# A hybrid decoder step: who issues two groups of loads, a second mask buffer, and where three small pieces of work stand in the order

## The chip, the cores and the metric

The kernel runs on one core of a Trainium2 chip. Its engines are TensorE (PE, matmuls; PEld is its loading of weights), VectorE (DVE), ScalarE (ACT), GpSimd (POOL) and SyncE (SP), which only starts transfers (DMAs). Each engine executes its own instructions in order, and waits where one needs what another engine or a transfer has not delivered. PE, DVE, ACT and POOL work on tiles in on-chip memory; `dram` names and the names ending in S or D (`qS`, `usD`, `biasS`) are buffers in device memory.

The metric is the device time of one execution in microseconds (us); of several runs the median is taken. From one further execution there is a profile: a record of every instruction with its start, its length and what it waited for.

## The reference

One layer of a decoder with two kinds of heads, for a prompt of 1024 tokens and 8 single decode tokens with a paged cache of 4096 positions each (R = 1032 columns in all, model width D = 2048), in float32:

```python
h = rmsnorm(x)
p = h @ w_in                        # q, k, v, index q/k/weights, gates, mLSTM q/k/v ...
# sparse attention: every query keeps its 256 best keys by an index score
s = relu(einsum('bqhd,bld->bqlh', qi, ki))        # 16 index heads of 64
scores = einsum('bqlh,bqh->bql', s, wi) * IDX_SCALE
_, idx = top_k(where(causal, scores, -inf), 256)
att = softmax(q @ k[idx] * ATT_SCALE) @ v[idx]    # 8 heads, 2 KV heads of 128
# mLSTM heads: chunks of 64 tokens, state C (256 x 128), n, m for each of 4 heads
h_ml, C, n, m = mlstm_run(...)
mix = concat(att * silu(z_att), rms(h_ml) * w * sigmoid(o) * silu(z_ml))
y = rmsnorm(x + mix @ w_out) * final_norm_w
```

The 8 decode tokens do the same against keys gathered from the cache. The outputs are y, the new keys and values, and the mLSTM states.

## The kernel before

**Tiles and products.** A float32 product is made of three matmuls on a high and a low part of each operand (H and L): H·H, H·L and L·H. `wH` is a weight tile rounded to the short format (made by ACT, line 251), `wL` the remainder (by DVE, line 252); `wraw` is the weight as loaded. Some of the input projection, and the output projection, are done as 7 products of 2x2 blocks in place of 8, for which sums and differences of weight blocks and of activations are formed first.

**Stages**, by the trace's time. Up to some 180 us: activations are loaded, normalised and split, and the first columns projected. To 390 us: the value columns (matmuls of line 1579, weights of lines 1573 to 1575). To 955 us: the other columns (matmuls `pj` of line 1509, results taken over by DVE into `ev` at line 375 or 377). To 1640 us: gates, products with the pre-summed weights (line 1746) and mLSTM. Then the output projection, whose last part (from 1760 us) is the blocks of line 2096.

**Jobs beside the projection.** Between the matmuls of a column the loop steps three *lanes* of jobs. A job is a generator that yields a weight after each small piece of work, and `Lane.step` paces it so that it ends by its due time (counted in columns). What a job emits stands in program order among the projection's instructions; a scheduler may move instructions, those passed to `pin` keep their place. The change touches these:

- `job_index` (from line 457) computes index scores and picks the best 256. It loads the index queries in groups of four heads, a *quad* (`qi`, line 471: 24 loads of 256 KB, two buffers); PE multiplies them by the index keys `ki` (line 489), ACT applies the relu (line 491, tile `rl`, two buffers), DVE sums the heads into `s` (line 494). For two blocks of 128 queries at a time, a search over 31 bits finds the threshold (lines 527 to 550). Then a mask is made for each block q = 0, 1 (lines 554 to 566): `gt` for scores above, `eq` for equal ones, a scan that keeps the first of these, and the store of `gt` to `biasS`.
- `job_dscore` gathers the decode tokens' index keys from the cache: POOL issues 32 gathers `kp` (line 1001, three buffers), PE transposes and multiplies them (line 1023).
- `job_datt` (from line 1263) is the attention of the decode tokens: gathers `ck` and `cv` on POOL (line 1289); for each of 8 tokens two products with the query (DVE, line 1314), each followed by a reduction (line 1318).
- `job_usum` (lines 1418 to 1431) forms weight sums in device memory for 12 pairs of columns: four sums `usD[0..3, i]` for each pair i. SP copies a block (line 1424), then POOL issues a transfer that adds another block to it (line 1425). Sum 1 starts from a copy of sum 0, and sum 2 from a copy of sum 1. Four pairs run side by side, step by step.

`gate_stage` reads the sums with the loads of lines 1728 and 1733.

**Last stage.** For the weight blocks' sums POOL computes `tt` (line 2090 in `tsum`), ACT and DVE split them (lines 2080 and 2085), and the activations are split by lines 2006 and 2007. Small work is put into a list `late`, of which `spread` emits some entries after each step k: among them `square` (line 2116, a sum of squares of finished rows) and `scaled` (line 2123: POOL multiplies finished rows `yt` by the norm's weight `fnr`).

Of the kernel before, what the change touches and what calls it, by code (L numbers as in the profile page):

```python
# [8 lines left out]
F32 = mybir.dt.float32  # L9
F32R = mybir.dt.float32r  # L10
BF16 = mybir.dt.bfloat16
I32 = mybir.dt.int32
AF = mybir.ActivationFunctionType
OP = mybir.AluOpType
# [4 lines left out]
S = 1024  # L19
# [32 lines left out]
T_G = 37  # L52
# [6 lines left out]
NP = (NT - T_G) // 2  # L59
# [112 lines left out]
def body(tc, A, stop=None):  # L172
# [284 lines left out]
    def job_index(groups):  # L457
        with tc.tile_pool(name="ix", bufs=2) as px:
# [6 lines left out]
            qis = {}  # L465

            def load_q(n):
                if n < len(quads):
                    i, h = quads[n]
                    qis[n] = px.tile([128, 4, 128], F32R, name="qi", bufs=2)  # L470
                    SY.dma_start(qis[n].bitcast(F32), qv[:, h:h + 4, i * 128:(i + 1) * 128])

            nq = 0
            load_q(0)
# [2 lines left out]
            for blocks in groups:  # L477
# [73 lines left out]
                V.tensor_tensor(tf, Tt.bitcast(F32), sgn, OP.mult)  # L551
                for q, i in enumerate(blocks):
                    W = (i + 1) * 128
                    gt = px.tile([128, S], BF16, name="gt", bufs=1)
                    eq = px.tile([128, S], BF16, name="eq", bufs=1)
                    s = Sv[q]
                    V.tensor_scalar(gt[:, :W], s[:, :W], sgn[:, q:q + 1], tf[:, q:q + 1], OP.mult, OP.is_gt)
                    V.tensor_scalar(eq[:, :W], s[:, :W], sgn[:, q:q + 1], tf[:, q:q + 1], OP.mult, OP.is_equal)
                    V.tensor_reduce(cnt[:, q:q + 1], gt[:, :W], AX.X, OP.add)
                    V.tensor_scalar(kp[:, q:q + 1], cnt[:, q:q + 1], -1.0, float(TOPK), OP.mult, OP.add)  # L560
                    yield W * 3.5
                    pin(V.tensor_tensor_scan(s[:, :W], eq[:, :W], eq[:, :W], 0.0, OP.add, OP.bypass))
                    V.scalar_tensor_tensor(eq[:, :W], s[:, :W], kp[:, q:q + 1], eq[:, :W], OP.is_le, OP.mult)
                    V.tensor_tensor(gt[:, :W], gt[:, :W], eq[:, :W], OP.add)
                    V.tensor_scalar(gt[:, :W], gt[:, :W], -1.0, POS, OP.add, OP.mult)
                    SY.dma_start(biasS[i], gt[:, :W])
                    yield W * 3.5
# [695 lines left out]
    def job_datt():  # L1263
        with tc.tile_pool(name="da", bufs=1, side="right") as pd:
# [41 lines left out]
            for b in range(NB):  # L1306
                if b + 2 < NB:
                    kgs.append(gather("ck", b + 2))
                if b + 2 < NB:
                    qbs.append(qload(b + 2))  # L1310
                qb, kg = qbs.pop(0), kgs.pop(0)
                for u in range(2):
                    jk = pd.tile([128, 8, 128], F32, name="jk", bufs=1)
                    v = V.tensor_tensor(jk.rearrange("p (v h) d -> p v h d", v=2),
                                    kg[u].rearrange("p (v d) -> p v d", v=2).unsqueeze(2).to_broadcast([128, 2, 4, 128]),
                                    qb.rearrange("p (v h) d -> p v h d", v=2), OP.mult)
                    pin(v)
                    V.tensor_reduce(lT[:, u, b * 8:b * 8 + 8], jk, AX.X, OP.add)
                V.tensor_tensor(kn[:, b, :].rearrange("p (v h) -> p v h", v=2),
                                dec[:, T_AQ:T_AQ + 8, b].rearrange("p (v h) -> p v h", v=2),  # L1320
                                dec[:, T_AK:T_AK + 2, b].unsqueeze(2).to_broadcast([128, 2, 4]), OP.mult)
                if b > 4:
                    vgs.append(gather("cv", b - 5))
                yield 5000
            for _ in range(4):
                yield 6000
            p2 = bank()
# [90 lines left out]
    def job_usum():  # L1418
        def steps(i):
            c1, c2 = T_G + 2 * i, T_G + 2 * i + 1  # L1420
            b11, b21 = (A["wa"][c1 - 9, y:y + 2] for y in (0, 2))
            b12, b22 = (A["wa"][c2 - 9, y:y + 2] for y in (0, 2))
            for n, base, more in ((0, b11, b12), (3, b22, b12), (1, usD[0, i], b22), (2, usD[1, i], b21)):
                yield lambda n=n, b=base: SY.dma_start(usD[n, i], b)
                yield lambda n=n, m=more: G.dma_start(usD[n, i], m, accum_op=OP.add, max_dma_last_dim=8192)  # L1425

        for i4 in range(0, NP, 4):
            for fs in zip(*(list(steps(i)) for i in range(i4, i4 + 4))):
                for f in fs:
                    pin(f())  # L1430
                    yield 1

    def att_free():
        return "datt" in lanes[1].done and "k" in mlc
# [7 lines left out]
    def ix_weight(blocks):  # L1442
# [13 lines left out]
                   Job("qrows", T_MQ + 0.5, 31, 1, job_qrows),  # L1456
                   Job("datt", T_MQ, T_G + 0.5, 10000 + 8 * 5000 + 34000 + 5 * 2500 + 8000 + 8000 + 5000, job_datt, ix_free),
                   Job("dml", T_G, T_G + 13, 28000 + 16 * 2500 + 5000, job_dml, dml_free)]),
             Lane([Job("usum", 19, T_G - 3, 8 * NP, job_usum)])]
    gateV = gateS.rearrange("(k p) r -> k p r", p=128)  # L1460
    mixb = [None] * KT
    first = []
# [685 lines left out]
    late = []  # L2148
    pw = None

    def spread(n):
        for f in late[:n]:
            f()
        del late[:n]
# [57 lines left out]
    def rows3(f, bs, g, tie=True):  # L2212
        late.extend(lambda b=b: f(b, g, True) if tie else f(b, g) for b in bs)
# [3 lines left out]
    for n in range(2):  # L2217
        ps = banks3(n)
        for k in range(8):
            with tc.high_priority():  # L2220
                T_ = tsplit(wblock(1, n, k, *single(n, k)), None, n > 0)
            blocks(ps, k, sP2[k], T_, LOW)
            spread(2)
            if not n and k < 4:
                pairprep(k)
            if n and k % 2:
                pairprep(4 + k // 2)
        for b in LOW:
            late.append(add(yt[b][n], ps[b], yt[b + HB * n][n]))
        if not n:  # L2230
            rows3(square, LOW, 0)
            rows3(scaled, LOW, 0)
    spread(9)

    sP7 = [None] * 8
# [1 line left out]
    for n in range(2):  # L2237
        p6, p4 = banks3(0), banks3(1)
        for k in range(8):
            with tc.high_priority():  # L2240
                b12 = wblock(0, 2 + n, k, pt, 6)
                b11 = wblock(0, n, k, pt, 6)
                b22 = wblock(1, 2 + n, k, pt, 6)
                b21 = wblock(1, n, k, wst, 2)
                t1 = tsum(b12, b11, G)
                SY.dma_start(t1D[n, k], t1)
                t2 = tsum(b22, t1, G)
                T2 = tsplit(t2, None, True)
                T4 = tsplit(tsum(T2[2], b21, V, OP.subtract, bank()))
            blocks(p6, k, pairs[k][0], T2, LOW)  # L2250
            blocks(p4, k, pairs[k][1], T4, LOW)
            spread(2)
            if n and k < 4:
                with tc.high_priority():
                    for j in (2 * k, 2 * k + 1):
                        sP7[j] = ssplit(quad(j)[0])
        with tc.high_priority():
            for b in LOW:
                V.tensor_tensor(yt[b][2 + n], p6[b], yt[b + HB][n], OP.add)
            for b in LOW:  # L2260
                V.tensor_tensor(yt[b + HB][n], yt[b][2 + n], p4[b], OP.subtract)
# [143 lines left out]
```

## Time and profile before

| | us |
|---|---|
| runs | 1994.36, 1994.91, 2005.22 |
| median | 1994.91 |
| profiled execution, its own time | 2002.27 |
| span of its instructions | 2000.1 |
| mean granted clock of TensorE, as a share of full speed | 0.986 |

| engine | busy us | instructions |
|---|---|---|
| PE | 1931.4 | 12710 |
| DVE | 1435.0 | 3280 |
| ACT | 900.7 | 1864 |
| POOL | 496.5 | 542 |

The span runs from the first to the last instruction. How a line of the profile is read: `L489` is line 489 of the kernel; `bank<-ki,qi` names what is written and what is read; `x2` is a count. In the list of waits, `A <- B: 11.1, 3, 4.7` says that A waited for B for 11.1 us in all, 3 times, 4.7 at the longest. In a time line the first number is the start, the second the length, and `[4.71 <-DMA qi<-qS]` says that the engine stood idle for 4.71 us before it and what ended that. `SPq` is SP's queue of transfers to be started: the length there is that of the starting, not of the transfer. "DMA to landing" is the time from the issue of a transfer to its end.

### The profile page before, as it was taken

To read this page: it belongs to the slowest core of one execution; us is meant where nothing else is said; L and a number is where in the kernel's file an instruction comes from. 1 tells how busy PE (TensorE), PEld (TensorE's weight loads), DVE (VectorE), ACT (ScalarE), POOL (GpSimd) and SP (SyncE) were. 2 spreads that over 40 slices of the span, in tenths; PEclk is the share of its full clock that TensorE was granted. 3 is DMA by queue.
4 is the path that set the end of the run, shared out by engine and by line. 5 is a ranking of instruction groups with operands and counts; after the bars stand their busy time and mean duration, and the time that the engine had idled before them with its cause. 6 is when DMAs were issued, how large, how long until landed. Compare 5 with 4: busy or idle time off the path is not lost. (4 is left out here: it accounts for less than half of the span.)

```text
span 2000.1 us, 35984 instructions
## 1 busy us (share of the span) xinstructions
PE 1931.4 (97%) x12710; PEld 1830.6 (92%) x12710; DVE 1435.0 (72%) x3280; ACT 900.7 (45%) x1864; POOL 496.5 (25%) x542
## 2 busy tenths in 40 slices
PE   9999998999999999989999999999999999998997
PEld 9998877899989899989899999999999999987886
DVE  8444888666858777867455658776778586788787
ACT  8122554345304345301155546554655444454655
POOL 0576776022310110033100000002123131106533
PEclk9999999999999999999999999999999999999999
DMA  7567565445875876387733597767789868898875
GB/s 259 149 196 209 172 186 158 124 155 181 242 206 153 216 195 164 101 237 223 228 98 99 164 300 215 231 192 244 230 252 318 205 240 271 271 344 280 278 253 191
DMA packets 250290, 421.31 MB, mean 211 GB/s; under 512 B 40101, under 2 KB 117221, under 8 KB 246269
## 3 DMA queue, kind: packets, MB, share of 16 engines
q1 hardware_dynamic: 231149, 347.68, 55.0%
q0 software_dynamic: 17664, 69.57, 13.9%
q8 instruction: 100, 1.64, 0.3%
q10 hardware_dynamic: 1296, 1.77, 0.3%
q14 instruction: 81, 0.66, 0.1%
HBM read 333.76 MB, written 135.48 MB: 235 GB/s over the span
## 5 line engine op out<-in xcount | busy, mean ns | idle before, releaser
L1509 PE MATMUL pj<-xH,wH 128*128 128x344 f32 (+1 forms) x1200 | 391.1, 329 | 14.1 <-DVE ev L375 8.7
L1509 PE MATMUL pj<-xL,wH 128*128 128x344 f32 (+1 forms) x1200 | 390.6, 326 | 0.2 <-DVE xL L309 0.2
L1509 PE MATMUL pj<-xH,wL 128*128 128x344 f32 (+1 forms) x1200 | 390.0, 326 | 0.0
L1746 PE MATMUL pj<-xH 128*128 128x258 f32 x1152 | 329.3, 286 | 2.5 <-DVE ev L1832 2.5
L1746 PE MATMUL pj<-xH,xL 128*128 128x258 f32 x1152 | 329.0, 286 | 0.0
L1746 PE MATMUL pj<-xL,xH 128*128 128x258 f32 x1152 | 328.7, 286 | 0.0
L1509 PEld LDWEIGHTS pj<-xH,wH 128*128 128x128 f32 x1200 | 227.6, 190 | 18.2 <-issue 13.9
L251 ACT CAST wH<-wraw 128x512 fp32r<-128x512 f32 (+2 forms) x183 | 109.9, 610 | 286.1 <-PE pj L1509 180.6
L1509 PEld LDWEIGHTS pj<-xL,wH 128*128 128x128 f32 x1200 | 227.9, 190 | 2.0 <-DVE xL L309 0.7
L1509 PEld LDWEIGHTS pj<-xH,wL 128*128 128x128 f32 x1200 | 227.8, 190 | 1.0
L1746 PEld LDWEIGHTS pj<-xH 128*128 128x128 f32 x1152 | 219.2, 190 | 5.3 <-issue 4.7
L1746 PEld LDWEIGHTS pj<-xL,xH 128*128 128x128 f32 x1152 | 219.2, 190 | 1.7 <-issue 0.4
L1746 PEld LDWEIGHTS pj<-xH,xL 128*128 128x128 f32 x1152 | 219.0, 190 | 1.8 <-issue 0.8
L252 DVE TENSOR_TENSOR wL<-wraw,wH 128x512 fp32r<-128x512 f32 (+2 forms) x183 | 129.7, 719 | 95.4 <-ACT wH L251 94.0
L538 ACT ACTIVATE eq<-eq 128x512 bf16<-128x512 bf16 (+2 forms) x93 | 78.5, 844 | 131.8 <-DVE eq L537 131.8
L2096 PE MATMUL pj<-wH,sH 128*128 128x512 f32 x336 | 131.2, 391 | 0.8 <-ACT wH L2080 0.4
L2096 PE MATMUL pj<-wH,sL 128*128 128x512 f32 x336 | 130.8, 389 | 0.0
L2096 PE MATMUL pj<-wL,sH 128*128 128x512 f32 x336 | 125.3, 392 | 4.9 <-DVE wL L2085 4.9
L491 ACT ACTIVATE rl<-bank 128x512 f32<-128x512 f32 (+2 forms) x160 | 80.1, 524 | 102.1 <-PE bank L489 67.0
L494 DVE SCALAR_TENSOR_TENSOR s<-rl,wiN,s 128x512 f32<-128x512 f32 (+2 forms) x150 | 101.9, 699 | 24.5 <-ACT rl L491 21.8
L1425 POOL DMA_DIRECT2D usD<-in_wa_dram x48 | 40.6, 1051 | 287.1 <-DMA usD<-in_wa_dram 169.7
L882 POOL CAST aH<-onec 128x4 fp32r<-128x4 f32 x16 | 6.0, 373 | 399.2 <-DVE onec L821 399.2
(506 smaller groups left out, 4828.9 us busy)
## 6 DMA issues: line engine op xcount, KB each, us to landing
wraw<-in_wt_dram SPq DMA_DIRECT2D x144, 256.0 KB
wraw<-in_wa_dram SPq DMA_DIRECT2D x110, 256.0 KB
usD<-in_wa_dram POOLq DMA_DIRECT2D x48, 512.0 KB, 8.5
wraw<-in_wo_dram SPq DMA_DIRECT2D x64, 256.0 KB
usD<-in_wa_dram SPq DMA_DIRECT2D x24, 512.0 KB
usD<-usD SPq DMA_DIRECT2D x24, 512.0 KB
xL<-xsD SPq DMA_DIRECT2D x40, 258.0 KB
ev<-spD SPq DMA_DIRECT2D x38, 258.0 KB
```

Of the source, the lines that this page charges most:

```text
L251: a = SC.copy(H[:, s, :cols], raw[:, s, :cols])
L252: return a, V.tensor_tensor(L[:, s, :cols], raw[:, s, :cols], H[:, s, :cols].bitcast(F32), OP.subtract)
L491: SC.activation(r[:, :cn], p[:, :cn], AF.Relu)
L494: v = V.scalar_tensor_tensor(s[:, c0:c0 + cn], r[:, :cn], wv, s[:, c0:c0 + cn], OP.mult, OP.add)
L538: SC.activation(junk2[:, :W1], junk2[:, :W1], AF.Copy, accum_out=cnt[:, 1:2])
L882: G.tensor_copy(aH[:, :, 256:258], onec)
L1425: yield lambda n=n, m=more: G.dma_start(usD[n, i], m, accum_op=OP.add, max_dma_last_dim=8192)
L1509: m = PE.matmul(ps[:cols, :cn], w_[:, k, :cols], x_[kk][:, c0:c0 + cn], start=(kk == ends[0] and z == 0), stop=(kk == ends[1] and z == 2))
L1746: PE.matmul(ps[c], w_[:, q, ks], x[y][:, c * CS:c * CS + CS], start=(first and q == 0 and k == 0 and z == 0), stop=(q == 1 and k == 3 and ...
L2096: PE.matmul(ps[b], S_[x][:, b * 128:b * 128 + 128], T_[y], start=(k == 0 and z == 0), stop=(k == 7 and z == 2))
```

## The change

Five edits. Lines behind 1312 move down by up to 12 in the new file, so that line 1424's copies are line 1427 there, line 1425's sums line 1430, and line 2123 is line 2134.

1. The 24 index-query loads are issued by ACT (`SC`) instead of SP (`SY`).
2. The mask of the second block of a pair is kept in the ring of the relu's output (`rl`, two buffers) instead of the single buffer `gt`.
3. In `job_datt` one yield of 5000 for each token becomes two of 2500, the first behind the first product and reduction.
4. In `job_usum` the copies of one sum to the next are issued by POOL (`G`) instead of SP, one pair behind; pairs follow each other instead of running four side by side. The job is due one column sooner.
5. In the last stage the scaling of the first finished rows is put into the list behind step 3 of the next loop instead of ahead of that loop.

```diff
@@ job_index
-                    SY.dma_start(qis[n].bitcast(F32), qv[:, h:h + 4, i * 128:(i + 1) * 128])
+                    SC.dma_start(qis[n].bitcast(F32), qv[:, h:h + 4, i * 128:(i + 1) * 128])
@@
-                    gt = px.tile([128, S], BF16, name="gt", bufs=1)
+                    gt = px.tile([128, S], BF16, name="rl" if q else "gt", bufs=1 + bool(q))
@@ job_datt
                     V.tensor_reduce(lT[:, u, b * 8:b * 8 + 8], jk, AX.X, OP.add)
+                    if not u:
+                        yield 2500
...
-                yield 5000
+                yield 2500
@@ job_usum
-            for n, base, more in ((0, b11, b12), (3, b22, b12), (1, usD[0, i], b22), (2, usD[1, i], b21)):
-                yield lambda n=n, b=base: SY.dma_start(usD[n, i], b)
-                yield lambda n=n, m=more: G.dma_start(usD[n, i], m, accum_op=OP.add, max_dma_last_dim=8192)
-
-        for i4 in range(0, NP, 4):
-            for fs in zip(*(list(steps(i)) for i in range(i4, i4 + 4))):
-                for f in fs:
+
+            def copy(n, src, queue):
+                return lambda: queue.dma_start(usD[n, i], src)
+
+            def plus(n, src):
+                return lambda: G.dma_start(usD[n, i], src, accum_op=OP.add, max_dma_last_dim=8192)
+
+            return ([copy(0, b11, SY), plus(0, b12), copy(3, b22, SY), plus(3, b12)],
+                    [copy(1, usD[0, i], G), plus(1, b22), copy(2, usD[1, i], G), plus(2, b21)])
+
+        late = []
+        for i in range(NP + 1):
+            now, more = steps(i) if i < NP else ([], [])
+            for n in range(4):
+                for f in now[n:n + 1] + late[n:n + 1]:
                     pin(f())
                     yield 1
+            late = more
@@ lanes
-             Lane([Job("usum", 19, T_G - 3, 8 * NP, job_usum)])]
+             Lane([Job("usum", 19, T_G - 4, 8 * NP, job_usum)])]
@@ last stage, loop over k
             rows3(square, LOW, 0)
-            rows3(scaled, LOW, 0)
     spread(9)
...
             blocks(p4, k, pairs[k][1], T4, LOW)
+            if not n and k == 3:
+                rows3(scaled, LOW, 0)
             spread(2)
```

POOL before, where the last gathers `kp` of `job_dscore` meet the first weight sums:

```order
183 L1001 DMA kp<-in_cik_dram,idx 128x512 x24
184 L1425 DMA usD<-in_wa_dram 64x2048
185 L1001 DMA kp<-in_cik_dram,idx 128x512
186 L1425 DMA usD<-in_wa_dram 64x2048
187 L1001 DMA kp<-in_cik_dram,idx 128x512
188 L1425 DMA usD<-in_wa_dram 64x2048 x2
189 L1001 DMA kp<-in_cik_dram,idx 128x512 x5
190 L1425 DMA usD<-in_wa_dram 64x2048
191 L1001 DMA kp<-in_cik_dram,idx 128x512
192 L1425 DMA usD<-in_wa_dram 64x2048 x38
```

The same place of POOL in the changed kernel:

```order
183 L1001 DMA kp<-in_cik_dram,idx 128x512 x21
184 L1430 DMA usD<-in_wa_dram 64x2048
185 L1001 DMA kp<-in_cik_dram,idx 128x512 x2
186 L1430 DMA usD<-in_wa_dram 64x2048
187 L1001 DMA kp<-in_cik_dram,idx 128x512
188 L1427 DMA usD<-usD 16x8192
189 L1001 DMA kp<-in_cik_dram,idx 128x512
190 L1430 DMA usD<-in_wa_dram 64x2048
191 L1001 DMA kp<-in_cik_dram,idx 128x512
192 L1430 DMA usD<-in_wa_dram 64x2048
193 L1001 DMA kp<-in_cik_dram,idx 128x512 x2
194 L1427 DMA usD<-usD 16x8192
```

The copies `usD<-usD` have come to POOL, and eleven gathers instead of eight stand behind the first transfer of the sums. Behind this place POOL repeats a copy and two sums.

SP before, at the last three index-query loads (among weights `wraw`, stores of `ev`, and copies of sums):

```order
298 L471 DMA qi<-qS 128x4x128
299 L1424 DMA usD<-in_wa_dram 16x8192
300 L248 DMA wraw<-in_wa_dram 128x512
301 L1424 DMA usD<-usD 16x8192
302 L471 DMA qi<-qS 128x4x128
303 L248 DMA wraw<-in_wa_dram 128x512
304 L1424 DMA usD<-usD 16x8192 x2
305 L248 DMA wraw<-in_wa_dram 128x512
306 L471 DMA qi<-qS 128x4x128
```

ACT in the changed kernel, at the same three loads:

```order
390 L491 ACTIVATE rl<-bank 128x384
391 L491 ACTIVATE rl<-bank 128x512
392 L471 DMA qi<-qS 128x4x128
393 L491 ACTIVATE rl<-bank 128x384
394 L491 ACTIVATE rl<-bank 128x512 x2
395 L251 CAST wH<-wraw 128x512
396 L491 ACTIVATE rl<-bank 128x512 x5
397 L471 DMA qi<-qS 128x4x128
398 L491 ACTIVATE rl<-bank 128x512
399 L251 CAST wH<-wraw 128x512
400 L491 ACTIVATE rl<-bank 128x512 x6
401 L471 DMA qi<-qS 128x4x128
```

The loads have left SP's queue, and stand behind relus of ACT.

DVE before, at the masks of the last pair of blocks (the weights' remainders `wL` and the evictions `ev` are the projection's):

```order
1242 L563 SCALAR_TENSOR_TENSOR eq<-s,sm,eq 128x896
1243 L564 TENSOR_TENSOR gt<-gt,eq 128x896
1244 L565 TENSOR_SCALAR gt<-gt 128x896
1245 L558 TENSOR_SCALAR eq<-s,sm 128x1024
1246 L252 TENSOR_TENSOR wL<-wraw,wH 128x512 x2
1247 L557 TENSOR_SCALAR gt<-s,sm 128x1024
1248 L559 TENSOR_REDUCE sm<-gt 128x1
1249 L562 SCALAR_TENSOR_TENSOR s<-eq 128x1024
```

The same place of DVE in the changed kernel:

```order
1226 L558 TENSOR_SCALAR eq<-s,sm 128x896
1227 L557 TENSOR_SCALAR rl<-s,sm 128x1024
1228 L559 TENSOR_REDUCE sm<-gt 128x1
1229 L252 TENSOR_TENSOR wL<-wraw,wH 128x512
1230 L562 SCALAR_TENSOR_TENSOR s<-eq 128x896
1231 L559 TENSOR_REDUCE sm<-rl 128x1
1232 L377 TENSOR_TENSOR ev<-pj_8118,rstd 128x344
```

The second mask (1024 wide) begins right behind the start of the first one, in the tile `rl`, ahead of two weight remainders that it stood behind before.

## The prediction

> **What bounds the kernel now.** I read the busy time of the engines first, then the list of what TensorE (PE) waited for, then stretches of 3 to 6 us behind its waits with the granted clock, and last the time line around each wait.
>
> ```profile
> PE 1931.4 (97%) x12710; PEld 1830.6 (92%) x12710; DVE 1435.0 (72%) x3280; ACT 900.7 (45%) x1864; POOL 496.5 (25%) x542
> PE bank L489 <- DMA qi<-qS: 11.1, 3, 4.7
> PE pj L1509 <- DVE ev L375: 8.7, 3, 6.1
> PE pj L2096 <- DVE wL L2085: 4.9, 4, 2.4
> PE pj L1509 <- DVE ev L377: 4.1, 1, 4.1
> PE bank L1023 <- DMA kp<-in_cik_dram,idx: 2.1, 1, 2.1
> 194.00:197.40 3.40, 3.40 (x18) 3.14 (x19) 2.76 (x5) 1.89 (x5) 3.28 (x4) 1.00 0.95 301
> 381.03:386.80 5.77, 5.77 (x17) 5.22 (x18) 1.76 (x3) 1.47 (x3) 0.00 (x0) 0.50 0.29 80
> 448.34:451.70 3.36, 3.36 (x14) 3.36 (x15) 1.21 (x2) 0.05 (x1) 0.94 (x1) 0.50 0.83 285
> 581.40:584.80 3.40, 3.40 (x14) 3.16 (x14) 2.39 (x11) 0.00 (x0) 0.00 (x0) 0.50 0.96 300
> 674.46:680.40 5.94, 5.94 (x18) 5.48 (x19) 1.96 (x6) 1.19 (x2) 2.36 (x3) 0.50 1.12 285
> 878.94:881.80 2.86, 2.86 (x10) 2.86 (x11) 0.61 (x2) 0.00 (x0) 0.00 (x0) 0.51 0.81 248
> 929.50:932.90 3.40, 3.40 (x15) 3.40 (x14) 3.40 (x6) 0.00 (x0) 0.00 (x0) 0.51 0.46 117
> ```
>
> PE is busy for 97% of the span. The change leaves the matmuls alone, so it can win only PE's waits and what they bring with them. The wait rows give the awaited tile, the sum in us, how often, and the longest; the five groups sum to 30.9 us. The stretches give their length, then the busy time of PE, weight loads, DVE, ACT and POOL, then PE's granted clock. In six of the seven PE is busy at a clock of 0.50 or 0.51: work there takes twice as long, so 5.8 us at 0.50 costs 2.9 more. Behind the wait that ends at 194.00 the clock is 1.00, so not every wait is followed by that.
>
> [...]
>
> **Index queries (line 471), 24 loads, from SP's queue to ACT's.**
>
> ```profile
> 368.11 4.15 SPq L471 DMA_DIRECT2D qi<-qS  x1
> 381.03 0.98 PE L489 MATMUL bank<-ki,qi 128*128 128x384 f32 x2 [3.27 <-DMA qi<-qS]
> 659.60 0.54 SPq L471 DMA_DIRECT2D qi<-qS  x1
> 674.46 1.19 PE L489 MATMUL bank<-ki,qi 128*128 128x512 f32 x2 [4.71 <-DMA qi<-qS]
> L2139 ACTq DMA_DIRECT2D out_yP_dram<-yt x6: 338/338/387, 1973.5 to 1992.9; - x6
> ```
>
> The load issued at 659.60 is used at 674.46, 14.9 us later; the one of 368.11, whose issue alone took 4.15, 12.9 later. Both stand in SP's queue behind weight loads and other copies, and a load put on a queue of its own starts when its buffer is free. To remove 3.3 and 4.7 us of lateness, it need not be fast; it need only be that much sooner. Term: the three waits, 11.1, and the clock behind two of them, 2.9 + 3.0: **-17.0**, bounds 0 and -17.0. ACT issues 24 loads; its own DMA issues take 0.34 us (min/median/max in ns), so 24 x 0.34 = 8 us on an engine that is busy 45% of the time. In the order of the changed kernel each load stands behind the evictions (line 491) that wait for the very matmuls that free its buffer, so it adds no wait of length to ACT; if it did, the weight casts (line 251) behind it would be late, and they are what DVE and then PE wait for.
>
> [...]
>
> **Second mask buffer (line 554), and sums copied by POOL (lines 1418 to 1431).** Both meet in two waits.
>
> ```profile
> 854.38 0.86 SPq L248 DMA_DIRECT2D wraw<-in_wa_dram  x1
> 863.36 0.47 SPq L1424 DMA_DIRECT2D usD<-usD  x1
> 863.92 0.53 SPq L566 DMA_DIRECT2D biasS<-gt  x1
> 870.36 0.69 DVE L252 TENSOR_TENSOR wL<-wraw,wH 128x512 fp32r<-128x512 f32 x1 [11.35 <-ACT wH L251]
> 871.53 0.81 DVE L557 TENSOR_SCALAR gt<-s,sm 128x1024 bf16<-128x1024 f32 x1 [0.48 <-DMA biasS<-gt]
> 878.28 0.51 DVE L375 SCALAR_TENSOR_TENSOR ev<-pj,rstd 128x344 f32<-128x344 f32 x1
> 878.94 0.63 PE L1509 MATMUL pj<-xH,wH 128*128 128x344 f32 x1 [6.07 <-DVE ev L375]
> 572.61 0.68 DVE L557 TENSOR_SCALAR gt<-s,sm 128x768 bf16<-128x768 f32 x1 [6.01 <-DMA biasS<-gt]
> SPq L1424 <- DMA usD<-in_wa_dram: 26.4, 5, 8.0
> ```
>
> From 855.2 to 863.36 SP stands at a copy that must wait for an accumulation to land (8.0 us, the longest of the five in the last row). The mask's store (line 566) and the next weights stand behind it. DVE idles 11.35 us for the weights, then begins the second mask, which waits for the store of the first out of the same buffer, and does all of it (871.53 to 878) ahead of the eviction PE waits for. Up to 572.61 DVE idles 6.01 for that store, and the mask then stands ahead of the eviction (line 377) for which PE waits 4.1. With its own buffer the second mask starts in DVE's idle time; with the copies on POOL, SP reaches the store and the weights sooner. Late next are the casts of the weights, which SP then also loads sooner. Term: 6.1 + 4.1 of waits, and the clock behind them, (2.9 + 3.4)/2 = 3.1: **-13.3**, bounds 0 and -13.3.
>
> What POOL takes over (the first landing row is that of the sums of line 1425, the second that of the gathers of line 1001):
>
> ```profile
> L1425 POOL DMA_DIRECT2D usD<-in_wa_dram x48: 772/958/2176, 493.3 to 913.3; - x48
> DMA to landing us min/median/max: 5.3/8.5/17.5
> POOL kp L1001 <- PE bank L1023: 130.2, 21, 33.3
> DMA to landing us min/median/max: 3.2/4.3/9.8
> L1728 SPq DMA_DIRECT2D wH<-usD x16: 370/385/592, 1127.7 to 1615.4; - x16
> ```
>
> 24 copies at the 0.96 us of an accumulation are 23 us more on an engine that is busy 25%. Per pair POOL waits for three landings in a row (copy, accumulation, copy): 3 x 8.5 = 26 us. Twelve pairs and one step more are 13 x 26 = 332 us, and the sums have from 439.95, where their first copies are issued, to the first read at 1127.7: not on the path, cost 0. What is queued behind those waits is the gathers of line 1001: POOL executes in order, and in the new order the last 11 of 32 stand among sums. Those already wait for PE (130.2 us in 21 waits), that is, for one of three buffers.
>
> ```profile
> 439.70 0.94 POOL L1001 DMA_INDIRECT kp<-in_cik_dram,idx  x1 [6.44 <-PE bank L1023]
> 439.95 1.21 SPq L1424 DMA_DIRECT2D usD<-in_wa_dram  x2
> ```
>
> The gather of 439.70 is the one that PE waits for at 448.34 (2.1, and 3.36 at half clock: 1.7). It took 8.6 us beside copies that SP issues two at a time; now they come singly. I take half of 3.8: **-1.9**, bounds 0 and -3.8. The gathers that are now held behind sums I put down, by the same row, as one and a half such waits, **+5.7**, bounds 0 and three of them, 11.4.
>
> **One yield made two (lines 1312 to 1324).**
>
> ```profile
> 920.74 0.69 DVE L252 TENSOR_TENSOR wL<-wraw,wH 128x512 fp32r<-128x512 f32 x1 [2.45 <-ACT wH L251]
> 925.11 1.23 DVE L1314 TENSOR_TENSOR jk<-ck,qb 128x1024 f32<-128x1024 f32 x1
> 928.64 0.40 PE L1509 MATMUL pj<-xH,wH 128*128 128x344 f32 x1 [2.44 <-DVE ev L375]
> ```
>
> The other wait for line 375 is that of 928.64. Before its eviction DVE runs the products (line 1314) and reductions (line 1318) of the decode attention, of 1.2 us each, and a weight remainder (line 252); behind it the clock is 0.51 for 3.4 us, which costs 1.7. A yield between the two products of a row block lets the eviction pass the second pair, 2.4 us. But the weights were late at 920.74 as well, so of 4.1 I take half, **-2.1**, bounds 0 and -4.1. No instruction is added.
>
> **Scaling of finished rows three steps later (line 2232).**
>
> ```profile
> 1804.80 1.63 POOL L2123 TENSOR_TENSOR yt<-yt,fnr 128x512 f32<-128x512 f32 x1
> L2007 DVE TENSOR_TENSOR sL<-a,sH x8: 550/1342/1647, 1805.8 to 1823.6; 128x384 fp32r<-128x384 f32 x8
> L2007 DVE TENSOR_TENSOR sL<-a,sH x25: 543/548/1639, 1834.9 to 1928.4; 128x384 fp32r<-128x384 f32 x25
> ```
>
> Three products of 1.63 us alternate with POOL's weight sums (line 2090) from 1804.80 on. Meanwhile DVE's subtraction at line 2007 takes a median of 1.34 us, against 0.55 later, and PE waits 4.9 in four places for DVE's weights (line 2085). Now POOL does its sums first, so these come 3 x 1.63 = 4.9 us sooner; but POOL stays as busy, and DVE as slow. I take half of the waits: **-2.5**, bounds 0 and -4.9. The rows' stores go later too, but still well over 100 us from the end at 2000.
>
> **Sum.** -17.0 - 13.3 - 1.9 + 5.7 - 2.1 - 2.5 = -31.1, from +11.4 (nothing won) to -43.1 (all won, no new wait). The profiled execution took 2002.3 us, 7.4 above the median of the runs, 1994.9. That gives 1971.2 in such an execution and 1963.8 from the median. Part of the 7.4 may be some of these very waits; I put 2 us of it there, so the forecast is **1966**, its own range 1952 (all won) to 1980 (half won).
>
> **Rivals.**
> - *Traffic, not the queue.* At 674.46 the DMA engines were fully busy (share 1.12); a load issued by ACT would arrive as late. For it: that stretch; against it: at 381.03 the share is 0.29 and the load was late all the same. The -17.0 goes: 1966 + 17 = 1983. Chance 0.10.
> - *The second mask does not pass.* It still runs in one go ahead of PE's eviction, only sooner, because evictions on DVE are in program order. The -13.3 goes: 1979. Chance 0.08.
> - *The waits move.* Where PE no longer waits for a query or a mask, it waits for weights, as in the 11.35 us above where ACT had them late. If four fifths of 31 come back: 1966 + 25 = 1991, no change. Chance 0.14.
> - *Slower: POOL holds the gathers.* Eleven gathers (line 1001) share POOL's order with instructions that wait 8.5 us for a landing. The one of 439.70 had to land in 8.6 us and was 2.1 late, so it had 6.5. With a landing of 4.3 (their median, beside 3.2 and 9.8) that leaves 2.2: from there on each us that POOL holds a gather stops PE. Held for 6.2 us each, three quarters of a landing, they come 4 us late; with 1.7 of clock that is 11 x 5.7 = 63 us: 1966 - 5.7 + 63 = 2023. Against it: POOL waits up to 33.3 us for PE before a gather, so most are issued with time in hand, and sums a pair apart have often landed when POOL gets there. Chance 0.08.
>
> **How the numbers follow.** Forecast 0.60, rivals 0.10, 0.08, 0.14, 0.08. The measurement of this kernel can tell about 0.5%, 10 us, from no change: faster is below 1985, slower above 2005. Forecast, traffic and mask give faster, 0.78; moved waits give the same, and a part of the traffic case lies near the bound, 0.15 in all; the held gathers give slower, 0.07. The range, 1948 to 1990, takes in the full win less 4 us for the scatter of runs, and reaches up into the moved waits; it leaves out the slower case, half of the moved waits and a little below.
>
> **What would show it.** Right: no wait of line 489 on the queries above 1 us, none of the two evictions behind a mask, SP's waits on the sums (26.4) gone, and fewer stretches at half clock before 940 us. Wrong: waits of line 1023 on gathers, at 450 to 550 us, that sum to over 10 us (held gathers); waits of line 489 still there with issue to use above 12 us (traffic); or new waits of line 1509 for weight casts (moved). If PE's busy time falls by 10 but its waits stay, only the clock has changed.

## The result

| | before | changed |
|---|---|---|
| median of 6 runs each, us | 1999.66 (1994.36 to 2005.22) | 1974.16 (1965.08 to 1976.02) |
| ratio | | 0.9865, 95% interval 0.9838 to 0.9892 |
| profiled span, us | 2000.1 | 1972.7 |
| mean granted clock | 0.986 | 0.993 |

The ratio is that of the means of the runs, and 1 - 0.9865 of 1999.7 is 27 us; the medians lie 25.5 apart. The forecast was a gain of 31 and a time of 1966, in a range of 1948 to 1990.

The page of the changed kernel, its list of PE's longest waits, and what POOL waited for (now with the sums' copies, line 1427, and sums, line 1430; the landing row is that of the gathers of line 1001):

```profile
PE 1917.7 (97%) x12710; PEld 1820.3 (92%) x12710; DVE 1433.6 (73%) x3280; ACT 900.2 (46%) x1864; POOL 508.5 (26%) x566
PE pj L2107 <- DVE wL L2096: 8.2, 4, 5.0
PE bank L1590 <- DVE wL L1586: 5.7, 7, 1.6
PE bank L1590 <- ACT wH L1585: 4.5, 2, 3.1
PE pj L1520 <- DVE ev L375: 1.9, 1, 1.9
POOL kp L1001 <- PE bank L1023: 116.8, 20, 30.5
POOL usD L1430 <- DMA usD<-in_wa_dram: 94.2, 11, 20.1
POOL usD L1427 <- DMA usD<-in_wa_dram: 73.4, 10, 8.3
DMA to landing us min/median/max: 3.3/3.7/14.1
```

No wait for a query is left, and of the evictions one wait of 1.9. PE's busy time fell by 13.7 with the same 12710 matmuls (1931.4 to 1917.7). That is the clock, by an estimate from its mean: at 0.986 some 28 us of the span were lost to it (0.014 of 2000.1), at 0.993 some 14 (0.007 of 1972.7). The span fell by 27.4, so the other 13.7 were waits. The last stage's wait for weights (line 2085 before, 2096 now) has grown, from 4.9 to 8.2.

I cut the span where PE's work changes: the *value* stage from the first matmul of line 1579 to the last of 1584, the *columns* from there to the first of line 1746, the *gates* to the first of line 2029, the *last* stage from the first of line 2096 to the end (line numbers of the kernel before). In the first profile the values run from 171 to 396 us, so the query waits of 194 and 381 us lie in the values, and the other waits of the prediction up to 929 us in the columns. All 14 profiles of this study in that cut (us; "idle" is PE's idle time in the columns, "half" the time at half clock there; the ratio is to the kernel before):

| kernel | ratio | values | columns | idle | half | gates | last |
|---|---|---|---|---|---|---|---|
| before | 1 | 224.4 | 558.9 | 19.7 | 23.9 | 700.4 | 249.6 |
| before again (e5) | | 222.1 | 555.6 | 18.7 | 17.1 | 698.3 | 252.5 |
| changed | 0.9865 | 219.2 | 534.4 | 2.3 | 3.4 | 690.5 | 258.4 |
| changed again (e9) | 0.9858 | 218.7 | 533.0 | 2.5 | 0 | 693.3 | 254.5 |
| queries only (e6) | 0.9976 | 221.8 | 547.2 | 11.2 | 13.7 | 693.5 | 254.6 |
| sums only (e7) | 0.9882 | 225.0 | 531.8 | 1.7 | 0 | 691.6 | 255.0 |
| changed, queries on SP (e1) | 0.9845 | 213.4 | 532.5 | 1.7 | 0 | 693.4 | 254.9 |
| the same again (e12) | 0.9850 | 218.5 | 531.8 | 1.0 | 0 | 693.2 | 255.9 |
| changed, one mask buffer (e2) | 0.9887 | 218.8 | 531.5 | 1.7 | 0 | 692.1 | 256.0 |
| changed, sums as before (e3) | 0.9961 | 220.1 | 546.8 | 13.1 | 10.2 | 692.4 | 254.7 |
| changed, scaling early (e4) | 0.9878 | 220.2 | 534.4 | 2.3 | 3.4 | 687.7 | 255.8 |
| changed, queries on SP, scaling early (e8) | 0.9864 | 215.9 | 532.4 | 1.7 | 0 | 689.7 | 254.2 |
| new order of sums, copies on SP (e10) | 0.9932 | 222.4 | 542.6 | 9.3 | 10.2 | 691.4 | 254.1 |
| old order of sums, copies on POOL (e11) | 1.0071 | 218.4 | 568.0 | 26.0 | 34.1 | 696.2 | 253.4 |

The gain lies in the columns: 555.6 to 558.9 before, 531.5 to 534.4 wherever the weight sums are in their new form.

### The profile page after: what moved, and what is told of

It is laid out like the page before. It is cut to its first block, busy times and chain, and to the rows that moved or that the text cites. A ratio compares the mean times of both kernels' runs of the same rounds, so it can differ in the third digit from the quotient of the medians.

```text
span 1972.7 us, 35929 instructions
## 1 busy us (share of the span) xinstructions
PE 1917.7 (97%) x12710; PEld 1820.3 (92%) x12710; DVE 1433.6 (73%) x3280; ACT 900.2 (46%) x1864; POOL 508.5 (26%) x566
## 4 chain that ended last, share of the span: by engine, by line
PE 75%; DMA 10%; DVE 8%; issue 3%; ACT 2%; SPq 1%; POOL 1%; ACTq 0%; POOLq 0%; DVEq 0%
PE pj L1520 24%; PE pj L1757 18%; PE pj L2107 5%; PE bank L2040 4%; PE bank L1757 3%; PE bank L489 3%; PE bank L637 2%; PE bank L690 2%; PE pj L1590 2%; PE bank L1520 2%; PE bank L681 1%; PE bank L1023 1%; DMA wraw<-in_wv_dram 1%; DVE wL L2096 1%; DMA spD<-ev 1%
## 5 line engine op out<-in xcount | busy, mean ns | idle before, releaser
L2107 PEld LDWEIGHTS pj<-wL,sH 128*128 128x128 f32 x336 | 63.7, 190 | 24.2 <-DVE wL L2096 11.0
## 6 DMA issues: line engine op xcount, KB each, us to landing
wraw<-in_wt_dram SPq DMA_DIRECT2D x144, 256.0 KB
wraw<-in_wa_dram SPq DMA_DIRECT2D x110, 256.0 KB
wraw<-in_wo_dram SPq DMA_DIRECT2D x64, 256.0 KB
```

The lines of the kernel that those rows point to most:

```text
L2107: PE.matmul(ps[b], S_[x][:, b * 128:b * 128 + 128], T_[y], start=(k == 0 and z == 0), stop=(k == 7 and z == 2))
```

## The experiments

**One part undone at a time.** Four runs undo, one at a time, three of the parts that the prediction priced; the split yield was not undone alone.

e1 and e12, the queries back on SP:

```diff
-                    SC.dma_start(qis[n].bitcast(F32), qv[:, h:h + 4, i * 128:(i + 1) * 128])
+                    SY.dma_start(qis[n].bitcast(F32), qv[:, h:h + 4, i * 128:(i + 1) * 128])
```

> The changed kernel with the index-query loads back on SP. Theory (place in SP's queue made the loads late): PE waits for the queries again, 5 to 11 us in two or three waits, with 3 to 6 us of half clock behind them; ratio to before 0.991 to 0.996, 8 to 17 us above the changed kernel's 0.9865. Rival (what freed SP were the weight-sum copies that left it, so the loads are on time there as well): no wait of line 489 on the queries above 1 us, ratio within 0.985 to 0.989.

> The changed kernel with the queries back on SP, on the same chip as the changed kernel itself. Theory (a query load issued by ACT does nothing for the columns once SP is free of the copies, and costs in the value stage, where ACT's casts are on the path): value stage 212 to 217 against 218 to 221, time 4 to 8 us below the changed kernel of this call. Rival (the 7 us between such pairs so far are scatter): within 3 us of it.

e2, one mask buffer again:

```diff
-                    gt = px.tile([128, S], BF16, name="rl" if q else "gt", bufs=1 + bool(q))
+                    gt = px.tile([128, S], BF16, name="gt", bufs=1)
```

> The changed kernel with one mask buffer again. Theory (both masks out of one buffer put the second in front of an eviction): DVE waits for the store of the first mask again (some 7 us in three waits), PE waits 4 us or more for an eviction of line 377 or 375 in one or two places, ratio 0.990 to 0.993. Rival (the store is now early enough, since SP no longer stands at a sum): DVE waits under 4 us, PE waits under 2 us, ratio 0.985 to 0.988.

e3, `job_usum` and its due time as before:

```diff
-            return ([copy(0, b11, SY), plus(0, b12), copy(3, b22, SY), plus(3, b12)],
-                    [copy(1, usD[0, i], G), plus(1, b22), copy(2, usD[1, i], G), plus(2, b21)])
...
+            for n, base, more in ((0, b11, b12), (3, b22, b12), (1, usD[0, i], b22), (2, usD[1, i], b21)):
+                yield lambda n=n, b=base: SY.dma_start(usD[n, i], b)
+                yield lambda n=n, m=more: G.dma_start(usD[n, i], m, accum_op=OP.add, max_dma_last_dim=8192)
+
+        for i4 in range(0, NP, 4):
+            for fs in zip(*(list(steps(i)) for i in range(i4, i4 + 4))):
...
-             Lane([Job("usum", 19, T_G - 4, 8 * NP, job_usum)])]
+             Lane([Job("usum", 19, T_G - 3, 8 * NP, job_usum)])]
```

> The changed kernel with the weight sums as before (copies by SP, four pairs side by side, due one column later). Theory (SP standing at a copy holds up weights): SP waits some 25 us on the sums again, weights come late, PE waits 3 to 8 us more in the column stage, ratio 0.989 to 0.993. Rival (with the second mask buffer and the queries gone from SP nothing urgent is behind those copies): column stage within 3 us of the changed kernel's 534.4, ratio 0.985 to 0.988.

Measured: e1 0.9845 (0.9821 to 0.9869), e2 0.9887 (0.9859 to 0.9915), e3 0.9961 (0.9942 to 0.9980). Rows of PE's waits, first of e1, then of e2 (all that either list has of an eviction by line 375 or of the queries), then of e3, with SP's wait at a copy there:

```profile
PE pj L1520 <- DVE ev L375: 1.6, 1, 1.6
PE bank L489 <- DMA qi<-qS: 1.5, 1, 1.5
```

```profile
PE bank L489 <- DMA qi<-qS: 1.4, 1, 1.4
PE pj L1520 <- DVE ev L375: 0.3, 1, 0.3
```

```profile
PE pj L1511 <- DVE ev L375: 10.3, 2, 8.6
SPq L1426 <- DMA usD<-in_wa_dram: 23.5, 2, 14.1
```

With the queries back on SP, or with one mask buffer, the columns are as short as in the changed kernel. So in e1 and e2 the rivals are nearer: with the sums in their new form, queries and masks are on time anyhow. Both miss their own figures narrowly (a wait of 1.5 and a ratio of 0.9845 in e1, a ratio of 0.9887 in e2). The wait of 1.5 in e1 is at the first query, near 193 us, as are the only query waits of e12 (2.5) and e8 (2.0). Undoing the sums brings back 12 to 15 us of the columns and 0.0096 of the 0.0135 in the ratio, more than either expectation of e3 had. On its own chip e12 came to 1962.6 beside 1966.1 for the changed kernel (e9), ranges 1959.0 to 1969.6 and 1959.8 to 1968.8: no difference that can be told, and the difference of 3.5 lies between its two expectations. The value stage of e1, 213.4, did not repeat in e12 (218.5), so that difference cannot be put down to the edit; the two ran on different chips.

e9 is the changed kernel itself, for that comparison.

> The changed kernel again, on the same chip as the next three, to compare them directly. Expected: ratio 0.985 to 0.989, column stage 530 to 536 us, value stage 218 to 221, gate stage 687 to 694.

It gave 0.9858 (0.9828 to 0.9888).

**One part alone, and the kernel before once more.** e5 is the kernel before, in one execution. e6 and e7 each put one edit of the change into it, with the lines shown in the section on the change:

```diff
@@ e6
-                    SY.dma_start(qis[n].bitcast(F32), qv[:, h:h + 4, i * 128:(i + 1) * 128])
+                    SC.dma_start(qis[n].bitcast(F32), qv[:, h:h + 4, i * 128:(i + 1) * 128])
@@ e7
+            return ([copy(0, b11, SY), plus(0, b12), copy(3, b22, SY), plus(3, b12)],
+                    [copy(1, usD[0, i], G), plus(1, b22), copy(2, usD[1, i], G), plus(2, b21)])
...
+             Lane([Job("usum", 19, T_G - 4, 8 * NP, job_usum)])]
```

> The kernel before, once more with a profile, to see how much of the first profile is chance. Theory (the column stage's waits belong to the order of the instructions): column stage 550 to 560 us with 15 to 20 us of PE waits again, at the same places (queries, masks, a gather). Rival (they are chance of one execution): column stage within 540 us, waits elsewhere. The order of PE in the gate stage is the same in all kernels: its length, 700.4 before and 688 to 693 in the five profiles since, should come out at 688 to 695 if the 700.4 was chance, at 700 if something of the kernel before reaches into it; the last stage likewise, 249.6 before and 255 to 258 since.

> The kernel before with the index queries on ACT's queue and nothing else. Theory now (the weight sums held up SP, and the queries only suffered from it): waits for queries gone, but the masks' waits stay and the value stage gets no shorter, ratio 0.993 to 1.000. Rival (the prediction's: the queries alone are worth 17 us): ratio 0.990 to 0.992.

> The kernel before with the new order and queue of the weight sums and nothing else: queries on SP, one mask buffer. Theory now: it has nearly the whole gain, column stage 530 to 537 us, no wait for a query above 1.5 us, ratio 0.983 to 0.988. Rival (the pieces add up as the prediction summed them): ratio 0.991 to 0.995, PE waits for queries of 4 us or more remain.

PE's waits in e5, before again; in e6, queries alone ("issue" stands for time in which the engine waited for nothing that the profile shows); and in e7, sums alone, with DVE's wait for the mask's store:

```profile
PE bank L489 <- DMA qi<-qS: 10.7, 3, 5.2
PE pj L1509 <- DVE ev L375: 8.2, 2, 4.7
PE pj L1509 <- DVE ev L377: 3.3, 1, 3.3
PE bank L1023 <- DMA kp<-in_cik_dram,idx: 2.0, 1, 2.0
```

```profile
PE pj L1509 <- DVE ev L375: 5.4, 2, 3.2
PE pj L1509 <- DVE ev L377: 3.7, 1, 3.7
PE bank L489 <- issue: 2.1, 1, 2.1
PE bank L1023 <- DMA kp<-in_cik_dram,idx: 2.0, 1, 2.0
PE bank L489 <- DMA ki<-kS: 1.3, 1, 1.3
```

```profile
PE bank L489 <- DMA qi<-qS: 2.7, 1, 2.7
PE pj L1518 <- DVE ev L375: 1.4, 1, 1.4
DVE gt L557 <- DMA biasS<-gt: 3.3, 2, 2.0
```

The waits of before come back in e5 at the same places, the sums of the rows within 0.8 us, single waits within 1.7: they belong to the kernel. The queries alone (ratio 0.9976, 0.9956 to 0.9997) remove their own row and leave the others; that is worth 0.0024 of 1995, 5 us, with an interval from 1 to 9, and the columns of the profile are 8 to 12 shorter. One of the three waits of that row is not won but renamed: near 194 us, where the kernel before waited 3.1 for the first query, PE now waits 2.1 and 1.3 for something else, and from 1.4 to 3.4 us stand at that place in all 14 profiles. The sums alone, 0.9882 (0.9858 to 0.9905), are worth 23.5 us. They remove the waits of 3 us and more for evictions, with one mask buffer, and the late query at 674 us, while the queries are still on SP; the one at 381 stays (2.7). The theory of the time holds in e6. In e7 it holds in the columns, while the ratio lies at the very edge of its range and the wait of 2.7 is above the 1.5 that it allowed.

**The last stage.** e4 puts the scaling back where it was, e8 that and the queries:

```diff
             rows3(square, LOW, 0)
+            rows3(scaled, LOW, 0)
...
-            if not n and k == 3:
-                rows3(scaled, LOW, 0)
```

> The changed kernel with the scaling of finished rows where it was before. Theory of the prediction (later scaling saves half of PE's waits in the last stage): last stage 2 to 3 us longer than the changed kernel's 258.4, ratio 0.987 to 0.989. Rival (the trace after has the last stage 8.8 us longer than before, so the later scaling lies in a worse place): last stage 248 to 252 us, ratio 0.981 to 0.984, faster than both kernels. Third: the 8.8 us are chance of one execution, last stage between and ratio as the changed kernel's.

> The changed kernel with the queries back on SP and the scaling of finished rows back where it was. If the queries on ACT cost something in the value stage (213.4 us with them on SP, 219 to 220 in four profiles with them on ACT), value stage 212 to 215 again; ratio 0.982 to 0.985 and at least as fast as the changed kernel. Rival (that difference was chance): value stage 218 to 221, ratio 0.986 to 0.988.

e4 gave 0.9878 (0.9853 to 0.9903), e8 0.9864 (0.9841 to 0.9886). The row of e4 for the wait that was 8.2 in the changed kernel:

```profile
PE pj L2107 <- DVE wL L2096: 6.7, 5, 3.4
```

Over all profiles the last stage takes 249.6 to 255.8 with early scaling (six) and 253.4 to 258.4 with late scaling (eight): means 253.6 and 255.2. The edit gains nothing there, and the 8.8 us between the first two profiles were mostly chance: the third expectation of e4. The value stage of e8, 215.9, lies between its two expectations.

**Why the sums.** Two things changed in them: who issues the copies, and in what order. (The due time went with the order in these runs and was not varied alone.) e10 keeps the new order and gives the copies back to SP; e11 keeps the old order and gives them to POOL.

```diff
@@ e10
-                    [copy(1, usD[0, i], G), plus(1, b22), copy(2, usD[1, i], G), plus(2, b21)])
+                    [copy(1, usD[0, i], SY), plus(1, b22), copy(2, usD[1, i], SY), plus(2, b21)])
@@ e11, against the loop of before
-                yield lambda n=n, b=base: SY.dma_start(usD[n, i], b)
+                yield lambda n=n, b=base: (SY if n in (0, 3) else G).dma_start(usD[n, i], b)
```

> The changed kernel's new order of the weight sums (a pair behind), but the copies of one sum to the next issued by SP. Theory A (what cost was SP standing in order at a copy that waits for a landing): SP waits on the sums again, 30 us or more, weights late, column stage 540 us or more, ratio 0.990 to 0.996. Theory B (what cost was the bursts of four copies and up to six sums at once; the order a pair behind cures that on any queue): column stage 530 to 536, ratio 0.985 to 0.989.

> The changed kernel with the old order of the weight sums (four pairs side by side, due one column later), but the copies of one sum to the next issued by POOL. Theory A (SP standing at the copies): SP is free, column stage 530 to 537, ratio 0.985 to 0.989. Theory B (bursts): four copies of 512 KB and four to six sums start together, landings of gathers and weights are late, column stage 540 us or more, ratio 0.990 to 0.996.

Measured: e10 0.9932 (0.9903 to 0.9961), e11 1.0071 (1.0046 to 1.0096). Neither half gives the whole gain, and with the second alone the kernel, its four other edits included, is slower than the kernel before. The same 480 us of the four kernels (stretches: length, busy time of PE, weight loads, DVE, ACT, POOL, then clock, busy share of the DMA engines, GB/s), first before, then changed, e10, e11:

```profile
440.00:920.00 480.00, 462.76 (x2920) 452.51 (x2920) 355.99 (x903) 166.63 (x320) 79.79 (x86) 0.98 0.71 195
```

```profile
440.00:920.00 480.00, 477.68 (x3053) 467.52 (x3052) 379.89 (x951) 170.61 (x328) 103.04 (x120) 1.00 0.74 204
```

```profile
440.00:920.00 480.00, 470.66 (x3006) 460.79 (x3005) 376.89 (x929) 169.81 (x325) 84.25 (x91) 0.99 0.73 202
```

```profile
440.00:920.00 480.00, 453.95 (x2838) 442.94 (x2837) 357.20 (x901) 164.17 (x315) 91.07 (x109) 0.96 0.70 194
```

PE gets through 3053 matmuls in the changed kernel and 2838 in e11, at about the same mean traffic. e10's largest wait, in the time lines of SP, DVE and PE:

```profile
847.48 0.33 SPq L248 DMA_DIRECT2D wraw<-in_wa_dram  x1
855.03 0.47 SPq L1427 DMA_DIRECT2D usD<-usD  x1
855.60 1.22 SPq L1274 DMA_DIRECT2D bias<-in_cst_dram  x1
861.82 0.35 DVE L1305 TENSOR_SCALAR bias<-bias,cc 64x256 f32<-64x256 f32 x1 [12.25 <-DMA bias<-in_cst_dram]
864.79 0.62 PE L1520 MATMUL pj<-xH,wH 128*128 128x344 f32 x1 [7.25 <-DVE ev L375]
SPq L1427 <- DMA usD<-in_wa_dram: 47.5, 8, 9.9
```

SP stands from 847.8 to 855.0 at a copy that waits for a sum to land. A small load for the decode attention (line 1274) stands behind it, DVE stands 12.25 us for that load, the next eviction stands behind DVE, and PE waits 7.25. In the changed kernel the same load is started at 844.39 and DVE does not wait for it. So a waiting copy on SP did harm here; in all SP waited 47.5 us for sums in this kernel. Theory A describes e10, but for the weights that it expected late: they were not, as rows further down show. In e11 SP issues none of these copies; the first and last of twelve transfers on POOL, and then what SP, the DMA engines, ACT and PE did meanwhile:

```profile
541.56 0.81 POOL L1427 DMA_DIRECT2D usD<-in_wa_dram  x1 [9.35 <-DMA usD<-usD]
...
566.40 0.77 POOL L1427 DMA_DIRECT2D usD<-in_wa_dram  x1 [2.53 <-DMA usD<-usD]
```

```profile
547.90 6.14 SPq L248 DMA_DIRECT2D wraw<-in_wa_dram  x2
553.00:567.50 14.50, 14.50 (x94) 14.38 (x93) 6.44 (x13) 0.00 (x0) 4.67 (x7) 1.00 1.03 322
567.54 0.62 ACT L251 CAST wH<-wraw 128x512 fp32r<-128x512 f32 x1 [14.59 <-DMA wraw<-in_wa_dram]
576.00 0.18 PE L1059 MATMUL bank<-cb,onesb 128*128 128x24 bf16 x1 [8.02 <-DVE cb L1057]
ACT wH L251 <- DMA wraw<-in_wa_dram: 89.9, 20, 15.4
```

Two weights of 256 KB are issued by 554.0, and ACT idles 14.59 us until 567.54 for one of them, while the DMA engines are fully busy (share 1.03, 322 GB/s): from 541.56 to 566.40 POOL starts twelve transfers of the sums, 512 KB each, in three groups of four. DVE is late with everything behind that weight, and PE waits 8.02. That is theory B, and by more than it had expected. ACT's waits for these weights in the kernel before, the changed one, e10 and e3, in this order:

```profile
ACT wH L251 <- DMA wraw<-in_wa_dram: 60.2, 17, 11.4
ACT wH L251 <- DMA wraw<-in_wa_dram: 35.0, 11, 7.1
ACT wH L251 <- DMA wraw<-in_wa_dram: 29.5, 10, 9.6
ACT wH L251 <- DMA wraw<-in_wa_dram: 87.5, 23, 8.6
```

They follow the order of the sums, whoever issues the copies: 58 to 90 us in the five profiles with the old order (87.5 with the copies on SP in e3, 89.9 on POOL in e11), 17 to 44 in the nine with the new one. So late weights go with the old order and not with the queue, and the standing of SP is a second harm, which e10 has without late weights. In e11 a query was late as well, though ACT issued it:

```profile
PE bank L489 <- DMA qi<-qS: 3.5, 1, 3.5
```

ACT starts that load at 651.1 and PE can use it at 659.0, at a busy share of the DMA engines of 1.06 (650.5 to 659.0).

Four pairs side by side make bursts; on SP the copies' own waiting spread them somewhat and blocked SP, on POOL they come faster. That it was the waiting on SP that spread them is a reading of these rows; no run varied it alone.

## Why the prediction was right, and where it was not

The time and the sign were right, and so, roughly, was the size of the gain in the columns. The terms for the columns sum to 4.7 + 3.0 (the query of 674 us and its clock) + 13.3 + 1.9 + 2.1 - 5.7 = 19.3, and 23.5 were measured (the mean of two profiles before, 557.2, less the mean of two after, 533.7); without the 5.7, which did not come, they are 25.0. The other two query waits lie in the values: 3.1 + 3.3 + 2.9 = 9.3 were forecast there and 4.3 measured, and one kernel's values differ by 5.1 from e1 to e12. That the total came within 4 us of the 31 is partly luck: the 5.7 that did not come and 7 us won in the gates that nobody forecast stand against the part missing in the values and a last stage that got 5 longer in place of 2.5 shorter. What failed is the division of the gain among the edits.

- *Queries, -17.0.* Wrong as the worth of this edit. Alone it gave 5 us, and taken out of the changed kernel it cost nothing. The step that failed is "both stand in SP's queue behind weight loads and other copies": it named the edit that would get them out of that queue, and did not ask which of the things ahead of them was slow. Ahead of the load of 659.60 SP starts a copy of the sums at 659.03, after 7.7 us in which it starts nothing. With the sums in their new form the late quad of 674 us is on time from SP as well (e1, e7). The wait of 381 us comes before the sums begin and is still there in e7. In the kernel before twelve small loads (lines 983 to 991) leave SP between 360.6 and 368.0, right ahead of that query; that they made it late is not shown. The queries on ACT cure it (e6; on ACT the last load of the changed kernel starts at 653.89, 0.03 us behind the last matmul that reads its buffer), and so do the edits that e8 has beyond e7 (second mask buffer and split yield), although the small loads stand ahead of the query there too.
- *Second mask buffer and sums, -13.3.* The waits went, but the sums alone take them away: with one buffer (e2, e7) no eviction waits over 1.4 us. The story of SP standing at a copy was right; the buffer's part in it was not needed once the sums had changed. In e3, with the second buffer and the sums as before, the wait at 580 us is gone too, while the one at 878, at the same matmul, is 8.6 long. Its own rival, 13 us lost if the mask did not pass, was wrong for the same reason.
- *Gather, -1.9.* The wait is there in both profiles of before and in e6, and 0.3 or nothing in all others, e3 with its old sums among them. It went whole. The sums alone take it away (e7), and so do other edits without them (e3); which of these is not settled.
- *Gathers held behind sums, +5.7, and the slower rival.* No wait of PE for a gather is left in the changed kernel, and their landings have a median of 3.7 beside 4.3. A slower kernel does exist, e11 at 1.0071, but through weights late in the traffic and not through held gathers. The rival was looked for in POOL's queue and lay in the DMA engines.
- *Split yield, -2.1.* Not tried alone. The wait at 928 is in before, e5 and e6 alone. It is gone in e7 without the yield, so the sums are enough, and in e3, with the yield, the second buffer and the sums as before; what the yield is worth stays open. The 7.4 us of e11 are at another matmul, some 20 us ahead of that place, behind a wait of ACT of 15.4 for a weight.
- *Scaling, -2.5.* Wrong: no gain, and perhaps 1 or 2 us lost, less than can be told.
- *The traffic rival.* Its price of 17 us was wrong: in e6 ACT's loads are on time beside the old sums. Its idea is partly borne out: once the sums are in their new form, it makes no difference that can be told which engine issues the queries (1966.1 in e9 and 1962.6 in e12). A queue that is standing is another matter: in e10 SP stood for 7.2 us at the copy (847.8 to 855.0), so the load behind it was some 7 us late because of its place in SP's order. And in e11, in the bursts, a load issued by ACT was late as this rival has it, by 3.5.
- *Clock.* The terms above hold 10.7 us for it (2.9 + 3.0 for the queries, 3.1 for masks and sums, half of 1.7 each for gather and yield), from half of each stretch at half clock, as if work took twice as long there. In the kernel before matmuls of 128x344 start every 0.29 us at 0.50 (879.36 to 881.37), and every 0.16 at 1.00 (868 to 870.5): 1.8 times, which makes some 9.7 of the 10.7, an estimate from these two stretches. PE's busy time fell by 13.7, in all stages together.

The 3 to 4 us between the columns' 23.5 and the 27 are a balance of other stages, by the means of two profiles each: the gates, where PE has the same 5559 matmuls (32 of them, of the decode attention, at other places in the order, which the expectation of e5 had taken for the same), got 7 shorter, the values 4, the last stage 5 longer. Gates of 698 and 700 appear only in the kernel before, 688 to 696 in all others, e6 among them, where PE's order is that of the kernel before. Why is not settled.

No version beats the changed kernel beyond doubt: with the queries left on SP (e1, e12) it is as fast, so that edit can be left out.

## What to carry to other kernels

Before several waits are charged to several edits, look for one thing that stands ahead of all of them: here five kinds of waits (the query of 674 us, two evictions, a gather, weights) went with one edit, the one to copies that came in bursts and waited for each other (e7). By these runs an instruction that waits for a landing belongs in a queue with nothing urgent behind it (SP's 7.2 us at a copy in e10 had PE wait 7.25), and the transfers that it starts belong one at a time (beside twelve from 541.56 to 566.40 in e11, ACT idled 14.59 us for a weight); here the new order alone brought 0.0029 of the 0.010 that the sums gave in the changed kernel (0.9961 to 0.9932 and 0.986; the first two have intervals that overlap), and the new queue alone lost 0.011. A row that vanishes from the list of waits is not yet won: look whether another stands at its place. Undo one edit at a time before believing a sum whose total is right.

## What the runs showed of the hardware

- The mean busy share of the DMA engines from 440 to 920 us said little about lateness here: 0.74 in the changed kernel and 0.70 in e11, but in e11 a weight of 256 KB issued by 554.04 was there only at 567.54, at least 13.5 us later, in a stretch at 1.03.
- The same order of PE's instructions took different times from one execution to another: the changed kernel's last stage 258.4 and 254.5 us (e9), and the value stage of one kernel 213.4 and 218.5 (e1 and e12, on different chips). Here two single profiles settled no difference of a stage below some 5 us, while waits of 2 us came back at their places, as that for the gather in before, e5 and e6 (2.1, 2.0, 2.0).
- In the columns the time at half clock went with PE's idle time: 23.9 us beside 19.7 in the kernel before, 34.1 beside 26.0 in e11, 3.4 or none wherever PE is idle for 2.5 or less.
